# Two-layer decoder trunk on one core: the base transfer of layer A's DMA-made weight sums is issued by SyncE instead of GpSimd

## The chip, the cores and the metric

The kernel runs on one core of a Trainium2 chip, in one launch. The metric is the device time of a run in microseconds; several runs of each kernel are compared by their median. One further execution of each kernel is taken by the hardware profiler: that is the profile, and its trace holds every instruction and transfer with its start and length. The engines are TensorE (PE), VectorE (DVE), ScalarE (ACT), GpSimd (POOL) and SyncE (SP). Each runs its own instructions in order and waits on semaphores for the others. Transfers (DMAs) are issued by SyncE and GpSimd, each on a queue of its own.

## The reference, cut to what matters

The reference is a two-layer decoder trunk on 512 tokens of width 2048, in float32. Layer A is a sparse attention: a projection `x @ w_in` gives queries, keys, values, a gate and the parts of an index, the index picks 128 keys for each query, and the attention's output, times the SiLU of the gate, goes through `w_o`.

```python
proj = x @ w_in
q, k, v, gate, iq, ik, iw = jnp.split(proj, SPLITS_A, axis=-1)
...
return (o * jax.nn.silu(gate)) @ w_o
```

Layer B is a stick-breaking attention over keys and values made once from the stream. After each layer come a layer norm and a gated embedding. The change is inside `x @ w_in` of layer A: in the blocks of the gate and the queries that are multiplied by a Strassen scheme.

## The kernel before

**Three products for one.** Every operand of a matmul is split into a high and a low part (`split`, lines 142 to 144: ScalarE copies the high part to the narrower float, VectorE subtracts it from the source), and `mm3` (lines 146 to 149) multiplies high by high, low by high and high by low. So each product is three matmuls, at lines 147, 148 and 149. Both engines are driven through a wrapper (`Paced`), so in the traces nearly all their work carries the line 118 or 116 of that wrapper, and is told apart by the names of its tiles.

**The stage.** Three blocks of 512 weight columns of layer A (`C_G + 512`, `C_G + 1024` and `C_Q + 1536`) go through `gemm_s`, one after the other. Each block is a Strassen product of 2 x 2 quarters: seven products in place of eight, each on sums of weight quarters and of quarters of x. The sums of x are made earlier (tile `ca`). The sums of weights are made here, by `added_items` (lines 484 to 522), in units. A unit is a pair of 128-row blocks of the weights, k and k + 8, over 512 columns; there are 8 units in a block and 24 in all, numbered u = 0 to 23. For each unit TensorE runs two row blocks of seven products of three matmuls, 128 x 256 in shape, into tile `m`.

**What a unit needs.** From the unit's four quarters q0 to q3 the four sums are s0 = q0 + q1, s1 = q0 + q2, s2 = s1 + q1 and s3 = s2 + q3. They lie in a place of 128 x 1024 floats, `st`. Two of them are always made by VectorE, s2 and s3 (lines 509 and 510). The other two are made in one of two ways:

- for units 0 to 6 and 21 to 23 by VectorE (`prepare`, lines 500 and 501);
- for units 7 to 20 by transfers (`send`, lines 488 to 494): a first one writes q0, read straight from the weights in HBM, into both s0 and s1 (line 492, the base of the sum, 256 KB); a second adds q1 onto s0 (line 493, 128 KB) and a third adds q2 onto s1 (line 494, 128 KB). The two adding transfers wait for the landing of the base.

Then, for each of the two row blocks of the unit, the three plain quarters are split into `wh` and `wl` and the four sums into `sh` and `sl`, 128 x 128 columns of each. These parts have three buffers each, so VectorE and ScalarE can be some half units ahead of TensorE.

**The places.** The units that use transfers take three places in turn, named `t3` (in the traces `t`) and two halves of `F[0]` (in the traces `f`). The sums of unit u stand where those of unit u - 3 stood, so a base may be written only when VectorE has split the sums of unit u - 3. The call for unit u + 2 is made while unit u is worked on.

**The weights themselves.** SyncE loads each unit's four quarters (line 231, tile `raw`, 512 KB), three buffers in turn. The load of unit u waits until the last plain quarters of unit u - 3 have been split. SyncE's queue holds in this stage nothing but these loads.

**GpSimd's queue.** In this stage it holds the base and the two adding transfers of each of the 14 units and two stores of 1 MB of a finished gate block (line 1220, `heldg`), and at its end the return of the held queries (lines 1214 and 1222).

**Between the blocks.** After a block its seven results are combined by VectorE and ScalarE while the next block runs (`combine_added`), and small steps (rounds of a top-k search, four sets of transposes of the keys into tile `kt`, the SiLU of the gate) are put between the matmuls at fixed numbers (`PUMPS`). After the third block the next product follows (tile `g`).

Of the kernel before, what the change touches and what calls it, by code (L numbers as in the profile page):

```python
# [19 lines left out]
H = T // 2  # L20
# [57 lines left out]
def trunk_kernel(  # L78
# [16 lines left out]
    nc = tc.nc  # L95
# [46 lines left out]
    def split(hi, lo, src, eng=dve):  # L142
        act.activation(hi, src, AF.Copy)
        return eng.tensor_tensor(lo, src, hi.bitcast(F32), ALU.subtract)
# [339 lines left out]
    def added_items(src, columns, places, wp, sent_ahead):  # L484

        n = len(columns) * 8

        def send(u):
            rows = src.rearrange("(k p) n -> k p n", p=128)
            c0, st = columns[u // 8], places[u].rearrange("p (i n) -> p i n", i=4)  # L490
            first, second = (rows[u % 8][:, c : c + H] for c in (c0, c0 + H))
            nc.gpsimd.dma_start(st[:, 0:2], first.unsqueeze(1).broadcast_to([128, 2, H]))
            nc.gpsimd.dma_start(st[:, 0], second, accum_op=ALU.add)
            nc.gpsimd.dma_start(st[:, 1], rows[u % 8 + 8][:, c0 : c0 + H], accum_op=ALU.add)

        def prepare(u):
            q = next_raw().rearrange("p a (b n) -> p (a b) n", b=2)
            st = places[u].rearrange("p (i n) -> p i n", i=4)
            if u not in sent_ahead:
                dve.tensor_tensor(st[:, 0], q[:, 0], q[:, 1], ALU.add)  # L500
                dve.tensor_tensor(st[:, 1], q[:, 0], q[:, 2], ALU.add)
            return q, st

        ready = None
        for u in range(n):
            q, st = ready or prepare(u)
            if u + 2 in sent_ahead:
                send(u + 2)
            dve.tensor_tensor(st[:, 2], st[:, 1], q[:, 1], ALU.add)
            dve.tensor_tensor(st[:, 3], st[:, 2], q[:, 3], ALU.add)  # L510
            for j in range(2):
                wh = top.tile([128, 512], F32R, name="wh", tag="wh", bufs=3)
                wl = top.tile([128, 512], F32R, name="wl", tag="wl", bufs=3)
                sh = wp.tile([128, 4, 128], F32R, name="sh", tag="sh", bufs=3)
                sl = wp.tile([128, 4, 128], F32R, name="sl", tag="sl", bufs=3)
                qh, ql = (w.rearrange("p (b c) -> p b c", b=4)[:, 0:3] for w in (wh, wl))
                cut = slice(j * 128, (j + 1) * 128)
                split(qh, ql, q[:, 1:4, cut])
                split(sh, sl, st[:, :, cut])
                if j and u + 1 < n:  # L520
                    ready = prepare(u + 1) if u % 8 else None
                yield [(qh[:, i], ql[:, i]) for i in range(3)] + [(sh[:, i], sl[:, i]) for i in (1, 2, 0, 3)]
# [737 lines left out]
    def scores(g, i):  # L1260
        w = 128 * (i + 1)
        s = slice(i * 128, w)
        sm = pb.tile([128, 4, 4], F32, name="sm", tag="sm", bufs=2)
        P[i] = pb.tile([128, 4, 384 + 128 * (i % 2)], F32, name="p", tag=f"p{i % 2}")
        for h in range(4):
            ps = spare("s")
            mm3(ps[:, :w], [q[:, s] for q in Q[g, h]], [k[:, :w] for k in K[g]], True, True)
            p = P[i][:, h, :w]
            least, rs, ri = (sm[:, h, j : j + 1] for j in range(3))
            with tc.issue_after(newest["soft" if h == 0 else "first"].ins) if "soft" in newest else ExitStack():  # L1270
                newest["first"] = dve.tensor_tensor_reduce(p, ps[:, :w], am[i], -HSCALE, -GONE, ALU.add, ALU.min, least)
            newest["exp"] = act.activation(p, p, AF.Exp, bias=least, scale=-1.0, accum_out=rs)
            dve.reciprocal(ri, rs)
            newest["soft"] = dve.tensor_scalar(p, p, ri, None, ALU.mult)
            if i == 3 and g < 3 and h == 3:
                if g == 1:
                    waiting.extend([lambda: None] * 5)
                waiting.extend(lambda h=h: following_query(g, h) for h in range(g == 1, 4))
            if (g, i, h) == (0, 3, 3):
                waiting.extend((*late, pack_rows, *[lambda: None] * 3, *turns))  # L1280
            if (g, i, h) == (3, 3, 3):
                waiting.extend(lambda n=n: split(*plain(n), fblock(n)) for n in (0, 8, 1, 9))
            yield
            if i == 3 and g == 1 and h == 1:
                following_query(1, 0)
# [107 lines left out]
    first = scores(0, 0)  # L1393
# [940 lines left out]
```

## Time and profile before

| | |
|---|---|
| median of 3 runs | 1829.78 us (1829.17 to 1831.68) |
| profiled execution | 1831.72 us |
| its span, first to last instruction | 1829.6 us |
| mean granted TensorE clock | 0.998 |
| busy: TensorE, VectorE, ScalarE, GpSimd | 99%, 84%, 57%, 4% |
| HBM read, written | 212.76 MB, 16.78 MB |

Each line of a profile view names an engine, an operation, a line of the kernel and the tiles as output<-input. Busy time is the time in which an engine had an instruction running; for TensorE the ends of matmuls are modelled, so that it is better read by the spacing of their starts. "A <- B" in a list of waits says that an instruction of A stood idle until B was done, with the total in us, the number of waits and the longest. The chain of waits follows the end of the program back from each instruction to what released it; a "DMA" piece in it is the time from issue to landing of a transfer. "issue" is time in which nothing that the profile shows was waited for. The granted clock is the share of full speed that TensorE was given.

### The profile page before, as it was taken

What the parts mean: (1) busy time and instruction counts of PE and PEld (TensorE: products, weight loads), DVE (VectorE), ACT (ScalarE), POOL (GpSimd) and SP (SyncE); (2) the same over time, 40 slices, a digit from 0 to 9 for tenths busy, and PEclk for the clock granted to TensorE, in tenths of its full rate; (3) what the DMA queues carried; (4) which work ended last, traced back from release to release, by engine and by line L of the source; (5) the groups of instructions that cost most, each with busy time, mean ns of one, the idle gap of its engine ahead of it and who ended that gap; (6) DMA issues with size and microseconds to landing.
All of it is one profiled execution on the core that took longest, in us unless ns stands there. A gap on an engine that the chain in (4) does not pass through costs nothing.

```text
span 1829.6 us, 28336 instructions
## 1 busy us (share of the span) xinstructions
PE 1813.4 (99%) x10231; PEld 1598.4 (87%) x10231; DVE 1535.4 (84%) x3057; ACT 1050.3 (57%) x1953; POOL 68.6 (4%) x117
## 2 busy tenths in 40 slices
PE   9999999989999999999999999999999999999999
PEld 9888888979888899888888899998888889988898
DVE  7888989858878899976568998888877889997997
ACT  4564354445776644575346444468888854457644
POOL 0000100331010000000000000000000000000000
PEclk9999999999999999999999999999999999999999
DMA  6524575666422344433437633322222244534453
GB/s 217 161 78 131 171 228 175 160 169 174 133 81 64 88 130 117 131 112 97 146 102 235 204 105 100 108 94 86 65 70 70 70 123 120 145 121 138 122 149 122
DMA packets 128892, 233.74 MB, mean 128 GB/s; under 512 B 11184, under 2 KB 44464, under 8 KB 127216
## 3 DMA queue, kind: packets, MB, share of 16 engines
q1 hardware_dynamic: 119936, 209.25, 38.1%
q0 software_dynamic: 8528, 22.29, 4.5%
q8 instruction: 80, 1.31, 0.3%
q14 instruction: 60, 0.49, 0.1%
q10 hardware_dynamic: 288, 0.39, 0.1%
HBM read 212.76 MB, written 16.78 MB: 125 GB/s over the span
## 4 chain that ended last, share of the span: by engine, by line
PE 93%; DMA 4%; DVE 1%; POOL 1%; issue 0%; ACT 0%; ACTq 0%; DVEq 0%
PE m L149 10%; PE m L148 10%; PE m L147 10%; PE g L147 10%; PE g L149 10%; PE g L148 10%; PE o L149 4%; PE o L148 4%; PE o L147 4%; DMA f<-w_in_a 3%; PE q L148 2%; PE q L149 2%; PE q L147 2%; PE iq L147 1%; PE iq L149 1%; PE iq L148 1%
## 5 line engine op out<-in xcount | busy, mean ns | idle before, releaser
L118 ACT ACTIVATE wh<-raw 128x512 fp32r<-128x512 f32 (+3 forms) x561 | 309.1, 552 | 368.9 <-PE g L148 116.9
L118 DVE TENSOR_TENSOR wl<-raw,wh 128x512 fp32r<-128x512 f32 (+3 forms) x560 | 330.7, 592 | 105.8 <-ACT wh L118 99.1
L147 PE MATMUL g<-xh,wh 128*128 128x512 f32 (+1 forms) x816 | 317.3, 389 | 0.0
L148 PE MATMUL g<-xl,wh 128*128 128x512 f32 (+1 forms) x816 | 314.5, 385 | 0.0
L149 PE MATMUL g<-xh,wl 128*128 128x512 f32 (+1 forms) x816 | 314.4, 385 | 0.0
L149 PEld LDWEIGHTS g<-xh,wl 128*128 128x128 f32 x816 | 153.3, 188 | 30.9
L147 PEld LDWEIGHTS g<-xh,wh 128*128 128x128 f32 x816 | 153.4, 188 | 29.1 <-ACT wk L116 0.3
L148 PEld LDWEIGHTS g<-xl,wh 128*128 128x128 f32 x816 | 153.5, 188 | 28.7
L118 ACT ACTIVATE sh<-f 128x512 fp32r<-128x512 f32 x123 | 76.7, 624 | 122.2 <-DVE f L118 117.1
L149 PE MATMUL m<-xh,wl 128*128 128x256 f32 x400 | 114.2, 286 | 7.0 <-DVE wl L118 7.0
L147 PE MATMUL m<-xh,wh 128*128 128x256 f32 x400 | 113.5, 284 | 1.3 <-ACT u L118 1.3
L148 PE MATMUL m<-xl,wh 128*128 128x256 f32 x400 | 113.3, 283 | 0.0
L147 PE MATMUL m<-c,sh 128*128 128x256 f32 x368 | 104.3, 283 | 0.0
L149 PE MATMUL m<-c,sl 128*128 128x256 f32 x368 | 104.3, 283 | 0.0
L148 PE MATMUL m<-c,sh 128*128 128x256 f32 x368 | 104.1, 283 | 0.0
L149 PE MATMUL o<-xh,wl 128*128 128x512 f32 x256 | 99.7, 389 | 0.0
L147 PE MATMUL o<-xh,wh 128*128 128x512 f32 x256 | 99.6, 389 | 0.0
L148 PE MATMUL o<-xl,wh 128*128 128x512 f32 x256 | 99.6, 389 | 0.0
L118 DVE TENSOR_TENSOR sl<-f,sh 128x512 fp32r<-128x512 f32 x123 | 84.7, 689 | 16.6 <-ACT sh L118 16.4
L147 PE MATMUL m<-xh,sh 128*128 128x256 f32 x336 | 95.8, 285 | 0.0
L148 PE MATMUL m<-xl,sh 128*128 128x256 f32 x336 | 95.5, 284 | 0.0
L149 PE MATMUL m<-xh,sl 128*128 128x256 f32 x336 | 95.5, 284 | 0.0
(463 smaller groups left out, 4836.8 us busy)
## 6 DMA issues: line engine op xcount, KB each, us to landing
raw<-w_in_a SPq DMA_DIRECT2D x95, 512.0 KB, 4.1
raw<-w_in_b SPq DMA_DIRECT2D x64, 512.0 KB, 3.8
raw<-w_ple_gate SPq DMA_DIRECT2D x44, 512.0 KB, 3.9
raw<-w_o_a SPq DMA_DIRECT2D x24, 512.0 KB, 4.7
raw<-w_o_b SPq DMA_DIRECT2D x24, 512.0 KB, 4.7
f<-w_in_a SPq DMA_DIRECT2D x16, 512.0 KB, 4.8
f<-w_kv_b SPq DMA_DIRECT2D x16, 512.0 KB, 4.4
raw<-w_kv_b SPq DMA_DIRECT2D x16, 512.0 KB, 4.4
```

The costliest lines, as they stand in the source:

```text
L118: ins = method(*args, **kw)
L147: pe.matmul(out, a[0], b[0], start=start, stop=False)
L148: pe.matmul(out, a[0], b[1], start=False, stop=False)
L149: pe.matmul(out, a[1], b[0], start=False, stop=stop)
```

## The change

Line 492 issues the base of a sum on SyncE's queue; the two adding transfers stay on GpSimd's. Nothing else is edited.

```diff
             first, second = (rows[u % 8][:, c : c + H] for c in (c0, c0 + H))
-            nc.gpsimd.dma_start(st[:, 0:2], first.unsqueeze(1).broadcast_to([128, 2, H]))
+            nc.sync.dma_start(st[:, 0:2], first.unsqueeze(1).broadcast_to([128, 2, H]))
             nc.gpsimd.dma_start(st[:, 0], second, accum_op=ALU.add)
             nc.gpsimd.dma_start(st[:, 1], rows[u % 8 + 8][:, c0 : c0 + H], accum_op=ALU.add)
```

The instructions of TensorE, VectorE and ScalarE stand in the same order as before. Those of GpSimd and SyncE move. GpSimd's queue before, in the middle of the stage, units 9 and 10 (`f_109` is `F[0]`, `t_1680` is `t3`; the names in brackets are the semaphores that a row waits for, DMASW those of GpSimd's transfers, DMAHW those of SyncE's):

```order
L492 DMA f_109<-w_in_a 128x2x256 [waits DMAHW1_49,DVE_49]
L493 DMA f_109<-w_in_a 128x256 [waits DMASW4_49,DMASW3_49]
L494 DMA f_109<-w_in_a 128x256
L492 DMA t_1680<-w_in_a 128x2x256 [waits DMASW7_49,DMASW6_49,DVE_49]
L493 DMA t_1680<-w_in_a 128x256 [waits DMASW6_49]
L494 DMA t_1680<-w_in_a 128x256
```

The same place of GpSimd's queue now, units 9 and 10 and the first row of unit 11:

```order
L493 DMA f_109<-w_in_a 128x256 [waits DMAHW6_49,DVE_49]
L494 DMA f_109<-w_in_a 128x256
L493 DMA t_1680<-w_in_a 128x256 [waits DMAHW0_49,DMASW5_49,DVE_49]
L494 DMA t_1680<-w_in_a 128x256 [waits DMASW6_49,DMASW4_49]
L493 DMA f_109<-w_in_a 128x256 [waits DMAHW2_49,DMASW7_49,DVE_49]
```

The base of unit 10 no longer stands behind the adding transfers of unit 9; the adding transfers wait for a transfer of SyncE's.

SyncE's queue at the same place before, the loads of the units 9 to 13:

```order
L231 DMA raw<-w_in_a 128x2x512 [waits DMAHW0_49,DVE_49]
L231 DMA raw<-w_in_a 128x2x512 [waits DMAHW1_49,DVE_49]
L231 DMA raw<-w_in_a 128x2x512 [waits DMAHW2_49,DVE_49]
L231 DMA raw<-w_in_a 128x2x512 [waits DMAHW3_49,DVE_49]
L231 DMA raw<-w_in_a 128x2x512 [waits DMAHW4_49,DVE_49]
```

and now, the loads and bases of the units 9 to 12:

```order
L231 DMA raw<-w_in_a 128x2x512 [waits DMAHW0_49,DVE_49]
L492 DMA f_109<-w_in_a 128x2x256 [waits DVE_49]
L231 DMA raw<-w_in_a 128x2x512 [waits DMAHW2_49,DVE_49]
L492 DMA t_1680<-w_in_a 128x2x256 [waits DMASW6_49,DMAHW1_49,DMASW5_49,DVE_49]
L231 DMA raw<-w_in_a 128x2x512 [waits DMAHW3_49,DVE_49]
L492 DMA f_109<-w_in_a 128x2x256 [waits DMASW7_49,DMAHW4_49,DMASW0_49,DVE_49]
L231 DMA raw<-w_in_a 128x2x512 [waits DMAHW5_49,DVE_49]
L492 DMA f_109<-w_in_a 128x2x256 [waits DMASW2_49,DMAHW6_49,DMASW1_49,DVE_49]
```

The base of a unit stands directly behind the load of the same unit (only that of unit 7, the first, stands ahead of its load), and ahead of the load of the next. In all 14 rows leave GpSimd's queue and 14 come to SyncE's.

## The prediction

> **What bounds the kernel now.** I read the page first, then the waits, then a table by stage, then the chain of waits inside the one stage that stands out.
>
> The page's busy times, and the longest waits of TensorE (engine, tile, line, what it waited for: us in total, times, longest):
>
> ```profile
> PE 1813.4 (99%) x10231; PEld 1598.4 (87%) x10231; DVE 1535.4 (84%) x3057; ACT 1050.3 (57%) x1953; POOL 68.6 (4%) x117
> PE m L149 <- DVE wl L118: 7.0, 5, 2.3
> PE kt L1184 <- ACT rp L118: 1.9, 2, 1.6
> PE m L147 <- ACT u L118: 1.3, 1, 1.3
> ```
>
> TensorE is busy 99% of the span, so the whole kernel is a TensorE kernel, and only a place where TensorE waits has anything to give. All three waits have tiles (m, kt, u) of layer A's three Strassen products, the stage the change touches. The table by stage of that stretch (busy time and instructions per engine, granted clock, DMA share, GB/s in 10 us each):
>
> ```profile
> 330.00:340.00 10.00, 10.00 (x86) 10.00 (x85) 9.35 (x18) 4.31 (x9) 3.65 (x5) 1.00 0.61 139
> 360.00:370.00 10.00, 9.91 (x82) 9.62 (x82) 5.17 (x11) 5.68 (x10) 2.50 (x4) 1.00 0.63 172
> 370.00:380.00 10.00, 7.83 (x60) 7.03 (x59) 4.62 (x9) 5.83 (x12) 4.75 (x7) 1.00 0.53 116
> 380.00:390.00 10.00, 8.51 (x67) 7.89 (x66) 6.14 (x13) 3.19 (x7) 3.28 (x5) 1.00 0.93 234
> 390.00:400.00 10.00, 7.10 (x54) 6.38 (x52) 5.62 (x12) 3.91 (x8) 2.64 (x4) 1.00 0.64 179
> 400.00:410.00 10.00, 8.36 (x55) 8.00 (x55) 6.62 (x13) 4.66 (x10) 5.14 (x8) 0.83 0.57 137
> 410.00:420.00 10.00, 7.67 (x53) 7.46 (x52) 5.68 (x12) 1.98 (x4) 4.46 (x6) 0.83 0.67 137
> ```
>
> In the first row TensorE starts 86 matmuls in 10 us; from 370 to 420 it starts 53 to 67, VectorE is only half busy, and the granted clock falls to 0.83. Something else is late. The chain of waits there (start, length, what) names it:
>
> ```profile
> 332.75 0.29 issue
> 333.03 3.94 DMA f<-w_in_a
> ...
> 338.38 4.90 DMA f<-w_in_a
> 343.28 0.28 issue
> 343.56 0.46 POOL f L493
> 344.14 0.54 POOL f L494
> 344.68 4.28 DMA t<-w_in_a
> ...
> 400.97 6.67 DMA f<-w_in_a
> ```
>
> One GpSimd queue carries everything: the base of a sum is issued (338.38) and lands 4.90 us later, L493 and L494 start their adding transfers, and only behind them (344.68) does the next base leave. Nothing overlaps except the last adds. From the base of unit 9 (338.38) to that of unit 18 (400.97) nine periods take 62.59 us, 6.95 us each.
>
> What TensorE needs per unit is less. Spacing of matmuls, a gap, a set of transposes, and the first rows of this stage and of the next, from the time line of TensorE:
>
> ```profile
> 307.69 0.28 PE L147 MATMUL m<-xh,wh 128*128 128x256 f32 x1
> ...
> 364.15 0.28 PE L149 MATMUL m<-xh,wl 128*128 128x256 f32 x1
> 364.31 0.66 PE L1184 MATMUL kt<-ident,f 128*128 128x128 f32 x4
> 364.73 0.36 PE L147 MATMUL m<-ca,sh 128*128 128x256 f32 x1
> ...
> 397.12 0.28 PE L147 MATMUL m<-xh,wh 128*128 128x256 f32 x1
> 397.24 0.28 PE L148 MATMUL m<-xl,wh 128*128 128x256 f32 x1
> 399.70 0.38 PE L149 MATMUL m<-xh,wl 128*128 128x256 f32 x1 [2.18 <-DVE wl L118]
> ...
> 447.58 0.40 PE L147 MATMUL g<-xh,wh 128*128 128x512 f32 x1
> ```
>
> A unit is two row blocks of seven products of three matmuls, 42 matmuls 0.12 us apart: 5.04 us. So 6.95 us of supply stand against 5.04 us of use, in the 14 units (7 to 20) whose sums are made by DMA.
>
> **What the stage loses today.** It runs from 307.69 to 447.58, 139.89 us. Its 24 units need 24 x 5.04 = 120.96 us. Four sets of key transposes cost 0.58 - 0.12 = 0.46 us each (364.15 to 364.73), 1.84 us. The rest, 139.89 - 120.96 - 1.84 = 17.1 us, is waiting and what follows from it: the gaps, ScalarE's copies queued behind splits that wait for sums, and matmuls at a lower clock right behind the long gaps. This is all that the change can give back.
>
> **The change part by part.** *What goes from GpSimd.* 14 instructions of L492, and with them the wait of a base for the adds before it. It was also GpSimd that sat out each landing before L493; it still does, but no base stands behind it.
>
> *What comes to SyncE.* The same 14 transfers, each behind the weight load of its own unit. A base waits until the place of three units before has been split, which is the last VectorE step of that unit; the load ahead of it waits for the split just before that one. What SyncE does today:
>
> ```profile
> SPq L231 <- DVE wl L118: 132.2, 24, 8.7
> ```
>
> All 24 loads already wait for that split, so the base blocks the queue only from the end of one split to the end of the next, 0.65 us (371.33 to 371.98, rows 370.77 and 371.29 below), and the load behind it waits for a split one unit (5 us) later anyway. That cover is large: I cost SyncE's blocking at nothing. Were it gone, a load would leave 0.65 us later, and it has two units in hand.
>
> *The new loop.* With three places in turn, the base of unit u+3 may go when unit u has been split. The loop over three units is: split ends, base issued, base lands, L493 and L494 issued, second adding transfer lands, VectorE's two sums and splits end. Its rows (VectorE's time line for one unit; landings of L492 and of L494, min/median/max; landings of loads and of a transfer of the base's size on SyncE's queue, medians):
>
> ```profile
> 368.20 0.89 DVE L118 TENSOR_TENSOR f<-f,raw 128x256 f32<-128x256 f32 x2 [3.43 <-issue]
> ...
> 370.77 0.56 DVE L118 TENSOR_TENSOR wl<-raw,wh 128x384 fp32r<-128x384 f32 x1 [0.24 <-ACT wh L118]
> 371.29 0.69 DVE L118 TENSOR_TENSOR sl<-f,sh 128x512 fp32r<-128x512 f32 x1
> DMA to landing us min/median/max: 3.4/5.7/7.0
> DMA to landing us min/median/max: 3.8/4.9/7.1
> raw<-w_in_a SPq DMA_DIRECT2D x95, 512.0 KB, 4.1
> raw<-w_o_a SPq DMA_DIRECT2D x24, 512.0 KB, 4.7
> raw<-w_o_a SPq DMA_DIRECT2D x16, 256.0 KB, 2.7
> ```
>
> - Split end to base issue: 0.29 us (332.75, "issue").
> - Base to landing: not in this trace on SyncE's queue. Bounds are 2.7 us (256 KB on that queue) and 7.0 us (the slowest L492). I take 5.4: it stands behind a 512 KB load (4.1 us) that left 0.65 us before, and 256 KB more cost 4.7 - 2.7 = 2.0 us; 4.1 - 0.65 + 2.0 = 5.4. That is also near the 4.90 and 4.28 of the chain's rows.
> - Landing to L493: 0.28; L493 to L494: 344.14 - 343.56 = 0.58.
> - L494 to landing: 4.9, the median; bounds 3.8 and 7.1.
> - Sums and splits: 368.20 to 371.98 (371.29 + 0.69), 3.8 us.
>
> Sum: 0.29 + 5.4 + 0.28 + 0.58 + 4.9 + 3.8 = 15.25 us for three units, 5.08 us a unit. That is TensorE's 5.04 but for 0.04 us; over units 10 to 20 it is 11 x 0.04 = 0.5 us, so nearly all of the 17.1 us comes back. With both fast ends it is 11.45 / 3 = 3.8; with both slow ends 19.05 / 3 = 6.35.
>
> *What is late next.* VectorE: from 360 to 420 it was busy 33.85 us (the six rows above) while 60 / 6.95 = 8.6 units passed, 3.9 us a unit, 78% of 5.04. It fits, but with less air, and ScalarE and VectorE run in order. Also a 1 MB store stands in GpSimd's queue, now directly between two adds:
>
> ```profile
> 379.58 1.21 POOL L1220 DMA_DIRECT2D heldg<-f x1
> heldg<-f POOLq DMA_DIRECT2D x2, 1024.0 KB, 7.1
> ```
>
> The adds of unit 15 follow it on the same queue; they can be later by 0 to 3 us once, partly covered by the splits that stand ready. For both I keep back 2 us (0 to 4). So 17.1 - 0.5 - 2 = 14.6 us.
>
> *A rule against it.* The DMA share in the six rows from 360 to 420 is 0.66 on average, 39.7 us of 60 for 8.6 units and one 1 MB store, so at most 4.6 us of all engines' time a unit, under 5.04 but near. The Trainium skill, "DMA: Bandwidth & Descriptors", section "Issuing engines are not separate DMA queues", says that transfers started from different engines end up on the same 16 engines and interleave, and that starting them from several saves only the time to initiate them. By that sentence alone the gain would be one issue slot a unit and no more, the second rival below. The trace speaks against reading it so here: what L493 holds up today is not issuing but landing:
>
> ```profile
> POOL f L493 <- DMA f<-w_in_a: 41.1, 9, 5.4
> POOL t L493 <- DMA t<-w_in_a: 15.1, 4, 4.7
> ```
>
> 56.2 us of GpSimd's queue in 13 waits, and no base could leave in them.
>
> **The sum.** The profiled execution took 1831.72 us (span 1829.6), 1.94 us above the median of 1829.78. Against its own time: 1831.72 - 14.6 = 1817.1. Nothing in the stage says that the median run loses less, so I take the 14.6 us off the median too: **1815.2 us**. The gain carries to the end, as TensorE has almost no other idle time to absorb it.
>
> **The rivals.** A difference under 0.2% (3.7 us) counts as none.
>
> 1. *Forecast, 0.70:* the loop falls to TensorE's pace; 1815.2, by itself 1812.7 (all 17.1 back) to 1819.
>
> 2. *The loop still bounds, at a smaller price, 0.18.* Base, load and adds now overlap, and each gets slower. With a base of 6.8 and adds of 6.6 the loop is 0.29 + 6.8 + 0.86 + 6.6 + 3.8 = 18.35, 6.1 us a unit. Over units 10 to 20 that loses 11 x 1.07 = 11.8 us; the splits enter it about half a unit ahead (2.5 us, an estimate: their parts have three buffers of half a unit, one in use, one being filled), so 9.3 stay and 7.8 are gained: 1822. If transfers took exactly today's time and only GpSimd's slot for the base (344.14 to 344.68, 0.54 us) were saved, 14 x 0.54 = 7.6 us says nearly the same, 1822.2. For it: landings grew from 3.94 to 6.67 along the chain. Against it: those bases were queued right behind the two adds of the unit before, and now are not.
>
> 3. *No change, 0.07.* The overlap is paid back in full: the loop must be 3 x 6.95 = 20.85, that is base and adds together 15.9 us, more than the slowest of both ever seen (14.1). 1829.8.
>
> 4. *Slower, 0.05.* The base waits in SyncE's ring behind its load while the adds share the engines with both. It decides from 15.9 us of landings on. If load and base both took twice as long (8.2 - 0.65 + 5.4 = 12.95) with the slowest add (7.1), the loop is 25.0, 8.3 us a unit, 1.4 over today's 6.95 for 9 units: 12 us slower, 1842. Against it: in the row from 380 to 390 the engines moved 234 GB/s, and 1 MB in 5.04 us asks for 208.
>
> That the change does not do what it says I rule out: the bases stand on SyncE's queue in the changed order, each right behind its load.
>
> **How the numbers follow.** Faster: cases 1 and 2, 0.88. Same: 0.07. Slower: 0.05. The likeliest case gives the time, 1815.2. The range has its low end at the full 17.1 us with a little over, 1812, and reaches up through case 2 to 1824, which leaves out cases 3 and 4 and the tail of 2.
>
> **What would show it.** Right: between 360 and 420 TensorE starts 82 or more matmuls in each 10 us at a clock of 1.00; the stage from the first m matmul to the first g matmul takes about 125 us, not 139.9; L493's waits lose their place in the chain of waits; bases leave about 5 us apart and land in 4 to 6 us. Wrong: if bases or adds land in more than 6.5 us (case 2 or worse), if SyncE's loads of the next unit come late, or if TensorE waits for ScalarE or VectorE in the stage where the sums had already landed, which would mean that 2 us was too little to keep back.

## The result and the profile after

The changed kernel takes 1813.61 us (median of 4 runs, 1813.17 to 1814.24), the kernel before, with its profiled execution counted in, 1830.73 us (median of 4 runs, 1829.17 to 1831.76). The ratio is 0.9907, with a 95% interval of 0.989 to 0.9925: faster by 0.9%, about 17 us. The prediction was 1815.2 us in a range of 1812 to 1824. The changed kernel's profiled execution took 1813.17 us with a span of 1811.5 us, 18.1 us shorter than the span before.

Busy times and all waits of TensorE in the changed kernel:

```profile
PE 1806.2 (100%) x10231; PEld 1594.3 (88%) x10231; DVE 1534.9 (85%) x3057; ACT 1052.2 (58%) x1953; POOL 58.1 (3%) x103
PE spun L167 <- PEq L2325: 0.8, 1, 0.8
PE iq L147 <- ACT wh L118: 0.4, 1, 0.4
```

The waits of the `m` and `kt` matmuls are all gone; what is left, 1.2 us, lies at the start of the kernel. The table by stage, the same stretch as before:

```profile
360.00:370.00 10.00, 10.00 (x86) 10.00 (x86) 7.02 (x13) 9.02 (x17) 3.62 (x5) 1.00 0.84 178
370.00:380.00 10.00, 10.00 (x87) 10.00 (x86) 7.75 (x16) 5.12 (x11) 2.30 (x3) 1.00 1.01 298
380.00:390.00 10.00, 10.00 (x85) 10.00 (x85) 7.99 (x16) 6.87 (x14) 3.48 (x4) 1.00 0.90 211
390.00:400.00 10.00, 10.00 (x86) 10.00 (x85) 8.70 (x17) 4.22 (x8) 3.50 (x4) 1.00 0.88 211
400.00:410.00 10.00, 10.00 (x86) 10.00 (x85) 7.38 (x15) 5.79 (x11) 2.31 (x3) 1.00 0.72 187
410.00:420.00 10.00, 10.00 (x85) 10.00 (x85) 9.29 (x21) 4.90 (x10) 0.56 (x1) 1.00 0.64 211
```

85 to 87 matmuls start in every 10 us, where 53 to 82 did, and the granted clock stays at 1.00, where it fell to 0.83. The DMA engines' share went up to 0.72 to 1.01 while transfers ran: the same bytes in less time. The ends of the stage on TensorE's time line, its first `m` matmul and the first `g` matmul of what follows:

```profile
307.44 0.28 PE L147 MATMUL m<-xh,wh 128*128 128x256 f32 x1
...
430.11 0.40 PE L147 MATMUL g<-xh,wh 128*128 128x512 f32 x1
```

122.67 us, against 139.89 before: 17.2 of the 18.1 us by which the span is shorter. Matmuls alone need 120.96 us; the four sets of transposes (0.44 us each in the chain of waits) make up the rest. SyncE's time line, loads (L231) and bases (L492) of units 9, 10 and 11, and the base of unit 20:

```profile
337.03 0.37 SPq L231 DMA_DIRECT2D raw<-w_in_a  x1
337.63 0.37 SPq L492 DMA_DIRECT2D f<-w_in_a  x1
341.48 0.37 SPq L231 DMA_DIRECT2D raw<-w_in_a  x1
342.13 0.37 SPq L492 DMA_DIRECT2D t<-w_in_a  x1
346.51 0.37 SPq L231 DMA_DIRECT2D raw<-w_in_a  x1
347.17 0.37 SPq L492 DMA_DIRECT2D f<-w_in_a  x1
...
395.27 0.37 SPq L492 DMA_DIRECT2D f<-w_in_a  x1
```

Each base leaves some 0.65 us behind its load, and from unit 9 (337.63) to unit 20 (395.27) eleven periods take 57.64 us, 5.24 us each. That is TensorE's pace, 5.04 us a unit with the four sets of transposes between. The prediction's 6.95 us was for the nine periods up to unit 18; the bases of units 18 and 19 left close together before (400.97 and 401.98), and the eleven periods that can be set beside 5.24 us end in GpSimd's time line of the kernel before with the base of unit 20:

```profile
401.98 1.11 POOL L492 DMA_DIRECT2D t<-w_in_a  x1
...
410.33 1.91 POOL L492 DMA_DIRECT2D f<-w_in_a  x1
```

From 338.38 to 410.33 they take 71.95 us, 6.54 us each, so that 14.3 of the 17.2 us lie between these two bases. In the changed kernel, GpSimd's time line in the middle of it (the pairs L493, L494 of units 13 and 14, the 1 MB store, the pair of unit 15), and the landings of L492 and of L494:

```profile
363.68 0.87 POOL L493 DMA_DIRECT2D t<-w_in_a  x1 [3.56 <-DMA t<-w_in_a]
364.22 1.21 POOL L494 DMA_DIRECT2D t<-w_in_a  x1
367.17 0.86 POOL L493 DMA_DIRECT2D f<-w_in_a  x1 [1.74 <-DMA f<-w_in_a]
367.72 1.20 POOL L494 DMA_DIRECT2D f<-w_in_a  x1
370.93 0.56 POOL L1220 DMA_DIRECT2D heldg<-f  x1 [2.01 <-ACT f L118]
373.61 0.85 POOL L493 DMA_DIRECT2D f<-w_in_a  x1 [2.11 <-DMA f<-w_in_a]
374.16 1.18 POOL L494 DMA_DIRECT2D f<-w_in_a  x1
DMA to landing us min/median/max: 2.8/4.6/7.0
DMA to landing us min/median/max: 4.0/5.2/6.6
```

GpSimd still sits out landings, 1.7 to 3.6 us in these rows and 5.8 us in the next pair (unit 16, at 381.18), but no base stands behind it: the base of the next unit need not wait for that.

### The profile page after: what moved, and what is told of

It is laid out like the page before. It is cut to its first block, busy times and chain, and to the rows that moved or that the text cites. A ratio compares the mean times of both kernels' runs of the same rounds, so it can differ in the third digit from the quotient of the medians.

```text
span 1811.5 us, 28365 instructions
## 1 busy us (share of the span) xinstructions
PE 1806.2 (100%) x10231; PEld 1594.3 (88%) x10231; DVE 1534.9 (85%) x3057; ACT 1052.2 (58%) x1953; POOL 58.1 (3%) x103
## 4 chain that ended last, share of the span: by engine, by line
PE 100%; DMA 0%; DVE 0%; ACT 0%; issue 0%
PE m L149 12%; PE m L147 12%; PE m L148 12%; PE g L147 10%; PE g L148 10%; PE g L149 10%; PE o L149 4%; PE o L148 4%; PE o L147 4%; PE q L148 2%; PE q L147 2%; PE q L149 2%; PE iq L149 1%; PE iq L147 1%; PE iq L148 1%; PE z L2127 1%
## 5 line engine op out<-in xcount | busy, mean ns | idle before, releaser
L118 DVE TENSOR_TENSOR sl<-f,sh 128x512 fp32r<-128x512 f32 x123 | 84.7, 689 | 15.4 <-ACT sh L118 15.2
```

What stands on the lines that cost most here:

```text
L118: ins = method(*args, **kw)
```

## The experiments

Two theories stood against each other. **Queue order:** the change helped because the base no longer stands in GpSimd's queue behind adds that wait for a landing. **Path:** it helped because a base over SyncE's queue is faster (4.6 us to landing against 5.7). A third idea, the **loop** through the three places (split, base, adds, sums, splits), was tested by its numbers.

**The old path in a new order.** The base stays on GpSimd, but stands ahead of the adds of the unit before. `add` holds the two adding transfers; `keep` pins the order of the program.

```diff
-            nc.gpsimd.dma_start(st[:, 0:2], ...)
-            nc.gpsimd.dma_start(st[:, 0], ..., accum_op=ALU.add)
-            nc.gpsimd.dma_start(st[:, 1], ..., accum_op=ALU.add)
+            keep(nc.gpsimd.dma_start(st[:, 0:2], ...))
...
             if u + 2 in sent_ahead:
                 send(u + 2)
+            if u + 1 in sent_ahead:
+                add(u + 1)
```

> The base stays on GpSimd's queue as before, but stands ahead of the two adds of the unit before instead of behind them, so that no base waits for another base's landing. Queue-order theory (what the change removed is the base's place behind adds that wait for a landing): the adds now stand behind a base in the same ring, about 2 us more for them, so a loop of 0.29 + 5 + 0.28 + 1.2 + 6.5 + 3.8 = 17 us for three units, 5.7 a unit, about 5 us lost in the stage against the changed kernel and 12 gained against the kernel before: 1818, between 1814 and 1821. Path theory (what helps is SyncE's path, whose bases land in 4.6 us where GpSimd's took 5.7): nothing gained, 1828 to 1831.

Measured: 1814.61 us, ratio 0.992 (0.9904 to 0.9936). GpSimd's time line (L498 and L499 are the adds here) and the ends of the stage:

```profile
342.40 0.75 POOL L492 DMA_DIRECT2D t<-w_in_a  x1 [2.25 <-DVE sl L118]
343.13 0.90 POOL L498 DMA_DIRECT2D f<-w_in_a  x1
343.71 1.19 POOL L499 DMA_DIRECT2D f<-w_in_a  x1
347.47 0.75 POOL L492 DMA_DIRECT2D f<-w_in_a  x1 [2.57 <-DVE sl L118]
```

```profile
307.16 0.28 PE L147 MATMUL m<-xh,wh 128*128 128x256 f32 x1
...
431.64 0.40 PE L147 MATMUL g<-xh,wh 128*128 128x512 f32 x1
```

The base waits for a place (VectorE's split) and for no landing; the adds behind it start at once in all units but the last, since their base landed meanwhile. The stage takes 124.48 us: 15.4 of the 17.2 us are there without SyncE (14.2 by the medians of that session, 1828.79 and 1814.61). It is better than the 1818 us that the queue-order theory gave, because the second add, the last to land, did not get slower behind a base: L499 lands in 4.8 us (median), and I had allowed 6.5. Only the first add did, 4.7 us against 3.2. The base too lands in 4.8 us here, on the same path on which it took 5.7. That this comes of not leaving just behind two adds fits, but is not shown by itself. The path theory said 1828 to 1831 here and falls as the main cause: the order alone is enough for most of the gain.

**The new path in the old order, first try.** The base goes over SyncE's queue, held back until GpSimd has issued the adds of the unit before, by a small transfer that reads a tile which GpSimd writes behind them.

```diff
+            if u > 7:
+                keep(nc.sync.dma_start(passed_out[u % 2], passed[:, u % 2 : u % 2 + 1]))
             nc.sync.dma_start(st[:, 0:2], ...)
...
+            keep(pool.memset(passed[:, (u + 1) % 2 : (u + 1) % 2 + 1], 0.0))
```

> The base goes over SyncE's queue as in the change, but may leave only when GpSimd has issued the adds of the unit before: GpSimd writes a small tile behind them, and a transfer of 512 bytes that reads it stands ahead of the base on SyncE's queue. That is the old order on the new path. Queue-order theory: the gain is gone; base 4.6 + 0.28 + 0.58 + about 1.5 for the small write and transfer = 7 us a unit, 1829 to 1838. Path theory: the gain stays, 1813 to 1817.

Measured: 1916.97 us, ratio 1.0483 (1.046 to 1.0506), far outside both. The landings by tile say why:

```profile
f<-w_in_a SPq DMA_DIRECT2D x9, 256.0 KB, 10.4
passed<-passed SPq DMA_DIRECT2D x13, 0.5 KB, 8.2
```

The small transfer, 4 bytes in each of 128 partitions, takes 8.2 us, and the base behind it on the queue 10.4. The run shows what a small transfer ahead of a large one costs, and nothing about the order.

**The new path in the old order, second try.** Now GpSimd writes one column of the place itself, which the base overwrites, so that the base has to wait for that write and no transfer is added.

```diff
+            if u > 7:
+                keep(pool.memset(st[:, 0, 0:1], 0.0))
             keep(nc.sync.dma_start(st[:, 0:2], ...))
...
```

> Old order on the new path once more, without a transfer of its own: GpSimd writes one column of the place of unit u behind the adds of unit u - 1, and the base of unit u, over SyncE's queue, overwrites it and so has to wait for that. (The small transfer of the second run took 8 us itself and held up the base in the ring, so that run was no measure of the order.) Queue-order theory: base 4.6, 0.28 and 0.58 to the adds, 0.57 behind the second, 0.75 for the small write and some 0.3 to the next base, 7.1 a unit as against 6.95 before: the gain is gone, 1828 to 1834. Path theory: the gain stays, 1813 to 1818.

Measured: 1825.24 us, ratio 0.9976 (0.9965 to 0.9987). GpSimd's time line (L497 the second add, L494 the small write), SyncE's (L495 the base), and the ends of the stage:

```profile
357.03 1.21 POOL L497 DMA_DIRECT2D f<-w_in_a  x1
357.57 0.77 POOL L494 MEMSET f<- 128x1 f32 x1
363.74 0.87 POOL L496 DMA_DIRECT2D f<-w_in_a  x1 [5.39 <-DMA f<-w_in_a]
```

```profile
340.34 0.37 SPq L495 DMA_DIRECT2D f<-w_in_a  x1
...
358.37 0.37 SPq L495 DMA_DIRECT2D f<-w_in_a  x1
...
410.57 0.37 SPq L495 DMA_DIRECT2D f<-w_in_a  x1
```

```profile
307.29 0.28 PE L147 MATMUL m<-xh,wh 128*128 128x256 f32 x1
...
441.51 0.40 PE L147 MATMUL g<-xh,wh 128*128 128x512 f32 x1
```

The base leaves at 358.37, behind adds of which the second started at 357.03, and the next adds wait 5.39 us for it: the old chain. From unit 9 to unit 20 a period is 70.23 / 11 = 6.38 us, against 6.54 in the kernel before and 5.24 in the changed one. The stage takes 134.2 us, so of 17.2 us only 5.7 are there (4.1 by the medians of that session, 1829.31 and 1825.24). The time lies between the two expectations. The queue-order theory's, 1828 to 1834, was too slow, since a base on this path lands in 3.8 us (median) here, not 4.6.

The 5.7 us are not the path by itself, though. The small write is a step that the kernel before does not have: here the base leaves 1.34 us behind the second add (357.03 to 358.37), there 0.54 us (344.14 to 344.68). Without these 0.8 us a period would be some 5.6 us, an estimate (6.38 - 0.8). So the path alone may be worth more than 5.7 us, and how much more no run shows. What is shown is that the order alone gives 15.4, the path with this write 5.7, and both together 17.2. The first two do not add up to the third, as they shorten the same chain and TensorE's pace caps the sum.

**The supply rate.** The kernel before in every respect, but only units 7, 9, ... 19 have sums made by transfers.

```diff
-    added = added_items(..., range(7, 21))
+    added = added_items(..., range(7, 21, 2))
```

> The kernel before, base on GpSimd in the old order, but only every second unit from 7 to 19 has its sums made by transfers, VectorE makes the others. If the queue's rate (6.95 us for each set of sums) is the bound, it now has 10.1 us of TensorE's time for each, and the whole gain is there with no change of queue: 1813 to 1816. If each set of sums in the old order costs its own fixed delay (17 us over 14 sets, 1.2 us), half stays: 1820 to 1823.

Measured: 1813.43 us, ratio 0.9911 (0.9894 to 0.9929). GpSimd's time line, three bases:

```profile
338.00 0.75 POOL L492 DMA_DIRECT2D f<-w_in_a  x1 [7.94 <-DVE sl L118]
...
347.53 0.74 POOL L492 DMA_DIRECT2D f<-w_in_a  x1 [3.75 <-DVE sl L118]
...
389.57 0.75 POOL L492 DMA_DIRECT2D t<-w_in_a  x1 [3.10 <-DVE sl L118]
```

With two units of TensorE's time for each set the queue waits for VectorE, not the other way, and seven sets in the old order cost TensorE nothing: the stage takes 122.67 us (307.52 to 430.19), as with the change. So the old order has no fixed price for each set; it is a rate, and hurts only when more is asked of it. With half the transfers each also lands sooner (the base in 3.8 us, median, against 5.7), so the queue's rate here is not quite that of the kernel before.

**No transfers at all.** VectorE makes the sums of all 24 units.

```diff
-    added = added_items(..., range(7, 21))
+    added = added_items(..., range(0))
```

> The changed kernel with no sums made by transfers: VectorE makes all four sums in all 24 units, so that there is no loop through the DMA at all. VectorE was busy 48.1 of 60 us between 340 and 400 in the changed kernel, 80%; two more adds of 128 x 256 a unit are 0.67 us of 5.04, so 93%. If VectorE's work only had to fit: the same as the changed kernel, 1813 to 1815. If its order and ScalarE's turn do not fit at 93%: some waits of TensorE in the second and third block, 1816 to 1822. If the sums by DMA are what makes the stage possible: 1825 or more.

Measured: 1814.77 us, ratio 0.9919 (0.99 to 0.9937). Two rows of its table by stage:

```profile
360.00:370.00 10.00, 10.00 (x86) 10.00 (x85) 9.07 (x20) 8.07 (x15) 0.00 (x0) 1.00 0.38 107
390.00:400.00 10.00, 9.82 (x80) 9.45 (x79) 9.21 (x20) 4.84 (x11) 0.00 (x0) 1.00 0.36 106
```

VectorE is busy about 90%, and TensorE misses almost nothing (80 matmuls in one row). The stage takes 123.3 us (308.13 to 431.45), 0.7 more than with the change. So the sums by transfer, as they stood in the kernel before, cost some 15 us against having none (16.6 by the stage, 14.0 by the medians), and the change takes that cost away.

**A heavier base.** Four copies in place of two (512 KB), on the changed kernel.

```diff
-            nc.sync.dma_start(st[:, 0:2], first.unsqueeze(1).broadcast_to([128, 2, H]))
+            nc.sync.dma_start(st, first.unsqueeze(1).broadcast_to([128, 4, H]))
```

> The changed kernel with a base of four copies in place of two (512 KB; the two extra copies are written over by VectorE's sums). Loop theory (three places, so that base, adds and splits of one unit share three units of TensorE's time): the base lands 2.0 us later, the loop is 0.29 + 6.6 + 0.28 + 0.58 + 5.2 + 3.8 = 16.75, 5.6 us a unit, 0.55 over TensorE's pace in 11 units less 2.5 us ahead: 3.5 us slower than the changed kernel, 1817, up to 1820. Rival (any base off GpSimd's queue is hidden): 1813.6. Rival (the 16 DMA engines are at their end, since they would have to move 1.25 MB in 5.04 us, 260 GB/s): loads late as well, 1825 or more.

Measured: 1818.39 us, ratio 0.994 (0.9923 to 0.9956). Landing of the base, the row of the table in which TensorE lost most matmuls, and its longest wait:

```profile
DMA to landing us min/median/max: 3.6/5.8/8.8
390.00:400.00 10.00, 8.12 (x61) 7.31 (x61) 8.34 (x16) 5.53 (x11) 2.75 (x5) 1.00 0.99 256
PE m L147 <- ACT u L118: 1.3, 1, 1.3
```

The base is 1.2 us later (5.8 against 4.6), the stage 126.3 us (307.65 to 433.91), 3.6 us more. From unit 9 (337.85) to unit 20 (399.47) a period is 61.62 / 11 = 5.60 us, the loop theory's 5.6. Its 3.5 us came too, but nearly all in one place, behind the second block, and not spread over 11 units: there TensorE waits for ScalarE's copy of a result of that block (tile `u`, 392.79), which stands behind splits that had waited for their sums. So the agreement of size is partly luck. At a DMA share of 0.99 the waits show no split behind a load, and the 1825 us or more of the rival in which the engines are at their end did not come.

**Two places instead of three**, once on the changed kernel and once on the kernel before; the base is sent after the splits of the unit that frees its place.

```diff
-    places = ... + [(third, two[1], two[0])[n % 3] for n in range(14)] + ...
+    places = ... + [(third, two[1])[n % 2] for n in range(14)] + ...
-            if u + 2 in sent_ahead:
-                send(u + 2)
...
                     ready = prepare(u + 1) if u % 8 else None
+                if j and u + 2 in sent_ahead:
+                    send(u + 2)
```

> The changed kernel with two places in turn for units 7 to 20 instead of three. Loop theory: the same loop of about 14.8 us (0.29 + 4.6 + 0.28 + 0.58 + 5.2 + 3.8) now serves two units, 7.4 us a unit against TensorE's 5.04: 2.35 us lost in each of 12 units less 2.5 us ahead, about 26 us over the changed kernel, 1835 to 1842. Rival (the gain is the queue alone, a base that no longer waits): the third place is spare, 1814 to 1818.

> The kernel before (base on GpSimd) with two places in turn instead of three. Loop theory: with two places the loop through the places (7.4 to 7.8 us a unit) is longer than the one through GpSimd's queue (6.95), so the queue no longer decides, and this kernel and the changed kernel with two places take the same time within 6 us: 1836 to 1846. Rival (the queue costs its share on top of the places): 15 us or more over the changed kernel with two places, 1852 or more.

Measured: on the changed kernel 1843.82 us, ratio 1.0079 (1.0064 to 1.0094); on the kernel before 1842.94 us, ratio 1.0077 (1.0061 to 1.0094). SyncE's time line of the first, the bases of units 9 and 20, eleven periods apart:

```profile
341.90 0.37 SPq L492 DMA_DIRECT2D t<-w_in_a  x1
...
427.86 0.37 SPq L492 DMA_DIRECT2D f<-w_in_a  x1
```

85.96 / 11 = 7.8 us a unit, where the loop gave 7.4; so the first of the two came out 2 us above its range of 1835 to 1842. With two places the loop is longer than the queue's 6.95 us, and the change is worth nothing: the two kernels agree within 1 us. The third place is what lets the order pay.

**ScalarE's queue.** The base on the queue of an engine that also computes.

```diff
-            nc.sync.dma_start(st[:, 0:2], ...)
+            nc.scalar.dma_start(st[:, 0:2], ...)
```

> The changed kernel with the base on ScalarE's queue instead of SyncE's. It stands behind the last ScalarE copy of a unit and waits there for VectorE's last split, about 0.7 us, with the next unit's copies queued behind it. Queue-order theory: the base leaves at the same time, so the gain stays but for ScalarE's wait: about 1 us of ScalarE a unit; ScalarE was busy 63 of 110 us in the stage, so 1813 to 1817. Rival (a wait on a queue that feeds VectorE stops the splits): VectorE's 3.8 us for sums and splits grow by 1 us, the loop to 15.8, 5.25 us a unit, and TensorE waits at each unit: 1816 to 1824.

Measured: 1814.39 us, ratio 0.9917 (0.9902 to 0.9932). TensorE has no wait on an `m` tile, so ScalarE's waits are covered. SyncE's queue, ScalarE's, and GpSimd's in the order of the first run all do: in each the base does not stand behind the adds.

## Why the prediction was right, point by point

- **The loss in the stage** was put at 17.1 us; the stage is 17.2 us shorter, and nothing of it was given back later. Part of the closeness is luck. The 17.1 us was read from one execution of 1831.72 us and taken off a median of 1829.78, on the ground that the median run loses no less. The median gain is 16.2 us from 1829.78, and the profiled executions lie 18.55 us apart. The runs of the kernel before, beside this and the other experiments, lie between 1825.57 and 1833.70 us, the four of the changed one between 1813.17 and 1814.24.
- **6.95 us against 5.04 in 14 units** would be a loss of 26.7 us, which the prediction did not set beside its 17.1. Over units 9 to 20 the rate before is 6.54 us, and 71.95 - 57.64 = 14.3 us of the loss lie there.
- **GpSimd's queue as the bound**, with a base behind adds that wait for a landing: shown by the first, the third and the fourth run. The prediction, though, argued from the place in the queue only and did not say how much the other path is worth in the old order; that is 5.7 of the 17.2 us with a small write in the chain, and without it is not shown.
- **Blocking of SyncE** at nothing: the load-to-base step is 0.60 to 0.66 us in the rows, 0.65 was said, and the waits show no split of the stage behind a load.
- **The loop.** Base to landing was taken as 5.4 us and is 4.6; the second add as 4.9 and is 5.2. The sum, 0.29 + 4.6 + 0.28 + 0.58 + 5.2 + 3.8 = 14.75, is 4.9 us a unit instead of 5.08, under TensorE's pace. The 0.5 us of loss from it did not come.
- **What is late next.** 2 us were kept back for VectorE's order and the 1 MB store. That is the term that was mis-sized: it measured nothing. The store did stand between two pairs of adds (370.93, then 373.61), the second add of unit 15 was the slowest (6.6 us) and so was the base of unit 16 (7.0 us), both above the 6.5 us that the prediction named as a sign of being wrong, but the splits that stood ready covered them. Without these two terms, 0.5 and 2 us, the forecast would have been 1812.7, 0.9 us under the measured median, which is less than the runs scatter.
- **The rule against it.** The DMA share rose to about 0.9, as 4.6 us a unit in 5.04 said, and the first add landed later (4.8 us against 3.2), which fits transfers that get in each other's way. That did not bound the gain, which came from a queue that waited. The first run makes it plain: one queue, the same transfers, another order, 15.4 us. The Trainium skill ("DMA: Bandwidth & Descriptors", section "Issuing engines are not separate DMA queues") says that transfers from several engines run on the same 16 engines and that only the time to initiate them is saved; the trace agrees with the first half, and here more than the second was saved.
- **The rivals.** A loop that still bounds, with landings of 6.8 and 6.6: the medians are 4.6 and 5.2, so not here; with the heavier base (5.8 us) it begins. No change and slower are ruled out by the interval.

## What to carry to other kernels

A transfer that waits for a landing closes its queue for everything behind it (56.2 us of GpSimd's queue here), so read an in-order queue by what stands behind its waits: a chain of "DMA, issue, POOL, DMA" in the chain of waits is a queue used as a rate, here one set in 6.95 us against 5.04 us of need. Putting the next independent transfer ahead of the waiting one, or on another queue, gave nearly the same gain here, and only as long as there was a third place for it to land in. And when work has been handed to transfers to spare an engine, measure now and then what it costs not to: here VectorE alone was as fast within 1.2 us.

## What the runs showed that was not expected

- A transfer of 512 bytes to HBM, 4 bytes from each of 128 partitions, took 8.2 us to land (median of 13), and a 256 KB base right behind it on the same queue 10.4 us instead of 3.8 to 4.6.
- Of two adds issued directly behind a base on GpSimd's queue only the first was slower for it: 4.7 us (median), against 3.2 in the kernel before. The second, which lands last, took 4.8 against 4.9.
- With the DMA engines' share at 0.84 to 1.01 between 360 and 400 us, where it was 0.53 to 0.93 before, the base landed sooner (4.6 us against 5.7, median) and the second add hardly later (5.2 against 4.9); only the first add took longer (4.8 against 3.2).
- In the kernel before, TensorE's two longest gaps are 397.24 to 399.70 and 413.44 to 416.05. Right behind the second came some 3 us at a granted clock of 0.50, with matmuls 0.21 us apart in place of 0.12. The first was followed by two shorter gaps (to 401.35 and to 402.34), and the 3 us at 0.50 came only behind these. Together they cost about 3 us of the 17.2, an estimate (14 and 15 spacings that take 3.3 us each time in place of 1.7 and 1.8). A gap of 1.87 us (371.04 to 372.91) left the clock at 1.00, and so it stayed in the changed kernel, without such gaps.
